# Stick-breaking attention scores as three one-pass products of split q and k, and value products placed behind another block's scores

## The chip, the core and the metric

The kernel runs on one core of a Trainium2 chip. The metric is the device time of one execution in microseconds (us). Below, PE is the matrix engine (TensorE), PEld its weight loads, DVE the vector engine, ACT the scalar engine, POOL GpSimd, and SP the queue that issues the transfers (DMA).

## What is computed

One decoder layer: RMSNorm, an input projection, two groups of 16 heads side by side (a state-space group, SSD, and a stick-breaking attention group), an output projection, and a convolutional feed-forward part. There are 16 meta tokens and 1024 real ones, and all data is float32. The change touches only the attention group, with head width 64:

```python
zlog = einsum('bqhd,bkhd->bhqk', q_block, k) / sqrt(64)
log_beta = log_sigmoid(zlog)
log_keep = where(valid, log_beta - zlog, 0)          # log(1 - beta)
after    = cumsum(log_keep, reverse) - log_keep      # keys between s and t
w        = where(valid, exp(log_beta + after), 0)    # strictly causal
out      = einsum('bhqk,bkhd->bqhd', w, v)
```

The kernel works on probabilities and not on their logarithms: `kp` is sigmoid(-z), `bt` is sigmoid(z), a running product of `kp` from the right end gives the remaining stick, and the weight is `bt` times that product.

## The kernel before

**Matrix products.** A float32 operand is multiplied in one of two ways. In most of the kernel it is split in two float32r parts, the rounded value ("h", written by ACT) and the rest ("l", a subtraction on DVE or POOL), and three products h·h, l·h, h·l are added in PSUM; one of these is one pass over the moving columns. Small products take the float32 tiles as they are. The projections (`pj_...`, line 163) are of the first kind, with 128 contraction rows, and the scores `z` (L612), the transposes `tw` (L633) and the value products `av` (L647) of the second.

**Attention.** Heads are taken in eight pairs p = 0 to 7; the two heads of a pair lie on partitions 0 to 63 and 64 to 127. For each pair there are eight blocks i = 0 to 7 of 128 queries, and block i sees n = 16 + 128(i+1) keys. A block goes through five steps:

- `block_weights`: the scores in chunks of at most 512 keys (widths 144, 272, 400, then 2x264, 2x328, 2x392, 2x456, and 348+348+344 for i = 7). In one chunk, the product of head 0 uses partitions 0 to 63 and that of head 1 partitions 64 to 127. ACT makes `kp` and `bt` out of PSUM (L613, L614), DVE runs the two product scans (L617), and POOL multiplies (L619). The PSUM tiles `zz`, two in all, hold the chunks of `z` and also the transposes `tw`.
- `block_turn`: two blocks later, `bt` is transposed on PE (`tw`) and copied by ACT to `th` (L635).
- `block_mix`: one block later still, the value products `av` of the two heads, 64 output columns each (L647), and the copy to `ysc`.
- once for each pair, `edge_turn` and `edge_mix` (`twc`, `avc`) treat the keys at the block borders.
- between these stand steps of `fill`: the projections of the next pair's q, k and v. A step is half a projection chunk, 12 products, and at most three steps stand in one block. From the middle of pair 6 on there is no `fill` left, and steps of the output projection (`mo`, L783) stand there in some blocks.

In the loop over p and i, the order on PE is the order of the code (`manual_schedule` for PE alone). In it a block reads: scores of its first two chunks; one to three `fill` steps; the third chunk (i = 7 only); `block_mix` of an older block; `block_turn` of an older block; a `fill` step. The other engines' orders are set by the scheduler. The attention tiles lie in a pool `ap`, opened when the SSD part is closed, in memory which that part used until then; whoever first writes there waits for the last SSD transfers. In the SSD part, and through its end, the first pairs' projections already run.

Of the kernel before, what the change touches and what calls it, by code (L numbers as in the profile page):

```python
# [16 lines left out]
P = 128  # L17
# [3 lines left out]
NM = 16  # L21
L = NM + T
# [4 lines left out]
NT = T // P  # L27
# [24 lines left out]
def tile_layer(ctx: ExitStack, tc: tile.TileContext, x, meta, rows, parts,  # L52
               w_z, w_xbc, w_dt, w_q, w_k, w_v, w_out, w_up, w_down, out):
    nc = tc.nc
    mm = nc.tensor.matmul
# [139 lines left out]
    rp = roll.enter_context(tc.tile_pool(name="roll", bufs=2, side="right"))  # L195
# [5 lines left out]
    with tc.tile_pool(name="pre", bufs=3, side="right") as pre:  # L201
        gpre = row_bcast(pre, 0, D, "gpre")
        for i in range(NT + 1):
            nr = NM if i == 0 else P
            c0 = 0 if i == 0 else NM + (i - 1) * P
# [5 lines left out]
            r = rstd_of(pre, ss[:nr], 1, nr, f"pre{i}")  # L211
# [3 lines left out]
            for hf in range(2):  # L215
# [11 lines left out]
    halves = (slice(0, 64), slice(64, 128))  # L227
# [22 lines left out]

    def qkv_steps(p, post):
        q = rp.tile([P, L + 3], F32, tag="rq", name=f"q{p}", bufs=3)
        k = rp.tile([P, L], F32, tag="rk", name=f"k{p}", bufs=3)
        for dst, nm in ((q, "q"), (k, "k")):
            def ev(acc, c0, n, dst=dst):
                nc.scalar.activation(dst[:, c0:c0 + n], acc[:, :n], AF.Copy)

            yield from qkv_block(f"{nm}{p}", ev, p > 1 or (p, nm) == (1, "k"))
        vt = rp.tile([P, L], F32, tag="rt", name=f"vt{p}", bufs=1)

        def evv(acc, c0, n):
# [4 lines left out]
        heads[p] = q, k, v, vc  # L266
        yield from qkv_block(f"v{p}", evv, p > 0)

        def turn_v(part):
            tp = psum_tp(f"vtp{p}_{part}")  # L270
            for b in range(4):
                c0 = (4 * part + b) * P
                nc.tensor.transpose(tp[:, b, :], vt[:, c0:c0 + P], ident)
            nc.scalar.activation(v[:, 4 * part:4 * part + 4, :], tp, AF.Copy)

        def turn_edge():
            edge = rp.tile([P, NT, NM], F32, tag="edge", name=f"edge{p}", bufs=1)
            nc.vector.tensor_copy(edge[:, :NT - 1, :], vt[:, P:NT * P].rearrange("p (t c) -> p t c", c=P)[:, :, :NM])
            nc.vector.tensor_copy(edge[:, NT - 1, :], vt[:, T:L])
            tp = psum_tp(f"vtc{p}")  # L280
            nc.tensor.transpose(tp[:, 0, :], edge.rearrange("p t c -> p (t c)"), ident)
            nc.scalar.activation(vc, tp[:, 0, :], AF.Copy)
            for j in range(2):
                nc.vector.tensor_copy(meta_q[halves[j], p, 4 * p + 2 * j:4 * p + 2 * j + 2], q[halves[j], M0:NM])
            nc.vector.tensor_copy(meta_k[:, p, :], k[:, 0:NM])
            nc.sync.dma_start(out=mvd[:, p, :], in_=v[:NM, 0, :])

        post += [lambda: turn_v(0), lambda: turn_v(1), turn_edge]
# [17 lines left out]
    with tc.tile_pool(name="ssd", bufs=1, side="right") as sp:  # L306
# [114 lines left out]
        q, adt = e, s2  # L421
# [170 lines left out]
                                pattern=[[-NM * mul, NT], [col, 32]], channel_multiplier=mul)  # L592
    edges, ys_of = {}, {}

    def block_weights(p, i):
        q, k = heads[p][:2]
        nm = f"{p}_{i}"
        if i == 0:
            edges[p] = ap.tile([P, 2, NT, NM], F32, tag="cb", name=f"cb{p}", bufs=2)
            nc.gpsimd.memset(edges[p][:, :, :, NM - 1:], 0.0)  # L600
        t0, n = NM + i * P, NM + (i + 1) * P
        kpt = ap.tile([P, 2, L], F32, tag="kp", name=f"kp{nm}", bufs=2)
        btt = ap.tile([P, 2, L], F32, tag="bt", name=f"bt{nm}", bufs=3)
        kp, bt = kpt[:, :, 0:n], btt[:, :, 0:n]
        chunks = key_chunks(n)
        for ci, (a, w) in enumerate(chunks):
            if ci == 2:
                yield
            z = psum_zz(f"z{nm}_{ci}")
            for j in range(2):  # L610
                h = halves[j]
                mm(z[:, j, :w], q[h, t0:t0 + P], k[h, a:a + w], start=True, stop=True)  # L612
            nc.scalar.activation(kp[:, :, a:a + w], z[:, :, :w], AF.Sigmoid, scale=-QSCALE)  # L613
            nc.scalar.activation(bt[:, :, a:a + w], z[:, :, :w], AF.Sigmoid, scale=QSCALE)  # L614
        m = n - NM
        for j in range(2):
            nc.vector.tensor_tensor_scan(kp[:, j][:, ::-1], kp[:, j][:, ::-1], hold[:, L - n:L][:, ::-1], 0.0,  # L617
                                         op0=ALU.mult, op1=ALU.max)
            nc.gpsimd.tensor_tensor(bt[:, j, 0:m], bt[:, j, 0:m], kp[:, j, 1:m + 1], op=ALU.mult)  # L619
        nc.gpsimd.tensor_tensor(edges[p][:, :, i, 0:NM - 1], bt[:, :, m:n - 1], kp[:, :, m + 1:n], op=ALU.mult)  # L620
        turn.append((p, i, bt))
# [188 lines left out]
    for p in range(8):  # L810
        for i in range(NT):
            if p == 0 and i == 0:
                run(fill, 1)
            block = block_weights(p, i)
            next(block, None)
            if p > 0 and i == 3:
                edge_mix(p - 1, edge)
            run(fill, 1 + (i < 3))
            if p == 6 and i == 4:
                ahead = [raw_w(0, k, None if k % 3 == 0 and k < 6 else wp_f32(("wlo", "whi", "wlo")[k % 3], f"wora{k}"))  # L820
                         for k in range(8)]
            run(block)
            if mix:
                block_mix(*mix.pop(0))
            if len(turn) > 2:
                mix.append(block_turn(*turn.pop(0)))
            run(fill, int(p > 0 or i > 3))
            if p == 6 and i == 5:
                run(fill)
                xpool.close()  # L830
                w1pool = wo1.enter_context(tc.tile_pool(name="wo1", bufs=1, side="left"))
                wres = []
                halo = psum_mm("halo0")
                wsteps = wout_steps(w1pool, 0, ssd_g, wres, halo_y(w1pool, 0, ssd_g), halo, ahead)
            if p == 6 and i == 6:
                run(wsteps)
                halo_store(w1pool, 0, halo)
                ys1 = [split_y(wp, 0, 1, ("whi", "wlo", WB))]
                first = ssd_half(wres, ys1)
            elif p == 6 and i == 5:  # L840
                run(wsteps, 4)
            run(first, int(p == 7 and (i % 2 or i > 5) or p == 6 and i == 7))
            if p == 7 and 2 < i < 6:
                run(meta_steps, 1)
            if p == 0 and i == 2:
                token_rstd(r_ssd, ap, "a")
            if p > 0 and i == 2:
                edge = edge_turn(p - 1)
# [808 lines left out]
```

## Time and profile before

| | |
|---|---|
| median of three runs | 1810.84 us (1809.62 to 1811.23) |
| the profiled execution | 1810.72 us |
| its span, first to last instruction | 1809.0 us |
| outside the span | 1.72 us |
| mean granted PE clock | 0.988 |

The page gives for each engine its busy time. Groups of rows name a line, an engine, an operation, output and inputs, and the tile's partitions and elements. In the views by time a row has the start, the length, the engine, the line, the operation, and the number of instructions merged in it; in brackets stands how long the engine was idle before it, and what ended that. Matrix instructions overlap each other, so the distance from start to start says what one costs, and its length does not. A float32 product has two MATMUL records, a float32r product has one. The time from about 420 to 975 us is the attention.

### The profile page before, as it was taken

To read this page: it belongs to the slowest core of one execution; us is meant where nothing else is said; L and a number is where in the kernel's file an instruction comes from. 1 tells how busy PE (TensorE), PEld (TensorE's weight loads), DVE (VectorE), ACT (ScalarE), POOL (GpSimd) and SP (SyncE) were. 2 spreads that over 40 slices of the span, in tenths; PEclk is the share of its full clock that TensorE was granted. 3 is DMA by queue.
4 is the path that set the end of the run, shared out by engine and by line. 5 is a ranking of instruction groups with operands and counts; after the bars stand their busy time and mean duration, and the time that the engine had idled before them with its cause. 6 is when DMAs were issued, how large, how long until landed. Compare 5 with 4: busy or idle time off the path is not lost. (4 is left out here: it accounts for less than half of the span.)

```text
span 1809.0 us, 27308 instructions
## 1 busy us (share of the span) xinstructions
PE 1734.8 (96%) x10942; PEld 1490.1 (82%) x10942; DVE 1061.0 (59%) x1125; ACT 831.3 (46%) x1373; POOL 863.3 (48%) x613
## 2 busy tenths in 40 slices
PE   6999999999999999999889899899999999999997
PEld 5899889888888888887567578888899998888886
DVE  5651864873553454455731246766666666657988
ACT  5423563544565565565652334543333333344444
POOL 3213753585555565554752223277777776600001
PEclk9999999999999999999999899999999999999999
DMA  4124333231011011011212545222333332196344
GB/s 157 47 71 131 99 114 118 65 94 42 24 37 36 26 46 36 24 48 61 70 54 76 200 140 174 73 97 88 105 111 105 93 112 88 60 327 220 97 122 158
DMA packets 90547, 173.96 MB, mean 96 GB/s; under 512 B 10698, under 2 KB 35818, under 8 KB 90420
## 3 DMA queue, kind: packets, MB, share of 16 engines
q1 hardware_dynamic: 90420, 172.21, 29.7%
q8 instruction: 86, 1.41, 0.3%
q14 instruction: 41, 0.34, 0.1%
HBM read 122.39 MB, written 49.79 MB: 95 GB/s over the span
## 5 line engine op out<-in xcount | busy, mean ns | idle before, releaser
L617 DVE TENSOR_TENSOR_SCAN kp<-kp,hold 128x272 f32<-128x272 f32 (+7 forms) x128 | 206.8, 1657 | 194.7 <-ACT kp L613 104.5
L619 POOL TENSOR_TENSOR bt<-bt,kp 128x256 f32<-128x256 f32 (+7 forms) x128 | 215.0, 1697 | 189.2 <-DVE kp L617 132.9
L1022 POOL TENSOR_TENSOR wl<-wr,wh 128x1024 fp32r<-128x1024 f32 x44 | 110.7, 2524 | 40.7 <-ACT wh L1021 40.7
L1470 PE MATMUL dn<-dl,dh 128*128 128x512 f32 x308 | 119.9, 389 | 0.1
L1470 PE MATMUL dn<-dh 128*128 128x512 f32 x308 | 119.9, 389 | 0.0
L1470 PE MATMUL dn<-dh,dl 128*128 128x512 f32 x308 | 119.8, 389 | 0.0
L1516 POOL TENSOR_TENSOR fms<-fms,nhalf 128x1 f32<-128x1 f32 x8 | 8.5, 1060 | 225.7 <-DMA ar<-fda 186.0
L613 ACT ACTIVATE kp<-z 128x288 f32<-128x288 f32 (+6 forms) x112 | 82.8, 739 | 56.8 <-PE z L612 33.1
L1399 ACT ACTIVATE dh<-ar 128x512 fp32r<-128x512 f32 x77 | 48.7, 632 | 111.5 <-PE dn L1470 88.9
L612 PE MATMUL z<-k,q 64*128 64x144 f32 (+6 forms) x448 | 87.0, 488 | 13.3 <-ACT bt L614 6.0
L1021 ACT ACTIVATE wh<-wr 128x1024 fp32r<-128x1024 f32 x44 | 46.6, 1060 | 114.7 <-PE fX L1079 68.3
L1151 DVE SCALAR_TENSOR_TENSOR ga<-gr,pp,ga 128x1024 f32<-128x1024 f32 x44 | 71.3, 1622 | 34.8 <-ACT ga L1144 34.0
L635 ACT ACTIVATE th<-tw 128x1024 f32<-128x1024 f32 (+2 forms) x96 | 74.7, 814 | 34.9 <-PE tw L633 33.0
L614 ACT ACTIVATE bt<-z 128x288 f32<-128x288 f32 (+6 forms) x112 | 83.0, 741 | 0.0
L633 PE MATMUL tw<-ident,bt 128*128 128x128 f32 x576 | 78.8, 282 | 3.8 <-issue 2.8
L647 PE MATMUL av<-th,v 128*64 128x128 f32 x1152 | 78.3, 281 | 0.0
L647 PEld LDWEIGHTS av<-th,v 128*64 128x64 f32 x1152 | 62.8, 138 | 18.8 <-issue 17.9
L1400 DVE TENSOR_TENSOR dl<-ar,dh 128x512 fp32r<-128x512 f32 x77 | 53.3, 692 | 42.0 <-ACT dh L1399 42.0
L633 PEld LDWEIGHTS tw<-ident,bt 128*128 128x128 f32 x576 | 63.2, 143 | 15.6 <-issue 13.1
L612 PEld LDWEIGHTS z<-k,q 64*128 64x128 f32 x448 | 36.9, 187 | 41.8 <-issue 18.5
L1470 PEld LDWEIGHTS dn<-dh 128*128 128x128 f32 x308 | 57.8, 188 | 12.3 <-ACT dh L1399 0.3
L1470 PEld LDWEIGHTS dn<-dl,dh 128*128 128x128 f32 x308 | 57.8, 188 | 12.3 <-DVE dl L1400 0.4
(546 smaller groups left out, 5749.2 us busy)
## 6 DMA issues: line engine op xcount, KB each, us to landing
wr<-in_w_up SPq DMA_DIRECT2D x44, 512.0 KB
fds<-ga SPq DMA_DIRECT2D x44, 256.0 KB
b<-in_w_down SPq DMA_DIRECT2D x44, 256.0 KB
ar<-fds SPq DMA_DIRECT2D x44, 256.0 KB
fda<-ga SPq DMA_DIRECT2D x33, 256.0 KB
ar<-fda SPq DMA_DIRECT2D x33, 256.0 KB
yk<-yd SPq DMA_DIRECT2D x16, 512.0 KB
zd<-zt SPq DMA_DIRECT2D x8, 520.0 KB
```

The lines of the kernel that those rows point to most:

```text
L612: mm(z[:, j, :w], q[h, t0:t0 + P], k[h, a:a + w], start=True, stop=True)
L613: nc.scalar.activation(kp[:, :, a:a + w], z[:, :, :w], AF.Sigmoid, scale=-QSCALE)
L614: nc.scalar.activation(bt[:, :, a:a + w], z[:, :, :w], AF.Sigmoid, scale=QSCALE)
L617: nc.vector.tensor_tensor_scan(kp[:, j][:, ::-1], kp[:, j][:, ::-1], hold[:, L - n:L][:, ::-1], 0.0, op0=ALU.mult, op1=ALU.max)
L619: nc.gpsimd.tensor_tensor(bt[:, j, 0:m], bt[:, j, 0:m], kp[:, j, 1:m + 1], op=ALU.mult)
L633: nc.tensor.transpose(tw[:, j, b, :], bt[:, j, c0:c0 + P], ident)
L635: nc.scalar.activation(th[:, :, :nb, :], tw[:, :, :nb, :], AF.Copy)
L647: mm(av[halves[j], :], v[:, kb, halves[j]], th[:, j, b, :], start=kb == 0, stop=kb == i)
L1022: nc.gpsimd.tensor_tensor(l, raw, h.bitcast(F32), op=ALU.subtract)
L1151: nc.vector.scalar_tensor_tensor(v, self.g[jj][:, :, i:i + 256], fconv_w[:, j, i:i + 1], v, op0=ALU.mult, op1=ALU.add)
L1400: sub(lo[:, k], raw, hi[:, k].bitcast(F32), op=ALU.subtract)
L1470: mm(banks[t], u[:, 0, c], v[:, 1, :], start=(p == 0 and i == 0), stop=(p == NPR - 1 and i == 2))
```

## The change

Three things are changed.

- k is written by ACT as a float32r tile `kh`, and DVE subtracts it from the projection's PSUM tile to make `kl` (L259 of the new file): three subtractions for each pair. The copy of the meta keys becomes a sum of the two.
- For every block, DVE makes `qh` (a cast, L604) and `ql` (a subtraction, L605) of the block's 128 queries. This is issued one block ahead, behind the scores of the block before; for block (0, 0) it is issued at its start. The tiles lie in the pool `ap`.
- The scores of a chunk are three one-pass products for each head (qh·kh, ql·kh, qh·kl), the two heads in turn. `block_mix` stands directly behind the first two chunks of scores, ahead of `edge_mix` and the `fill` steps; it stood behind the whole block.

```diff
-        k = rp.tile([P, L], F32, tag="rk", name=f"k{p}", bufs=3)
-        for dst, nm in ((q, "q"), (k, "k")):
+        kh = rp.tile([P, L], F32R, tag="rk", name=f"kh{p}", bufs=3)
+        kl = rp.tile([P, L], F32R, tag="rkl", name=f"kl{p}", bufs=3)
+        for dst, nm in ((q, "q"), (kh, "k")):
             def ev(acc, c0, n, dst=dst):
                 nc.scalar.activation(dst[:, c0:c0 + n], acc[:, :n], AF.Copy)
+                if dst is kh:
+                    nc.vector.tensor_tensor(kl[:, c0:c0 + n], acc[:, :n], kh[:, c0:c0 + n].bitcast(F32), op=ALU.subtract)
...
-            nc.vector.tensor_copy(meta_k[:, p, :], k[:, 0:NM])
+            nc.vector.tensor_tensor(meta_k[:, p, :], kh[:, 0:NM].bitcast(F32), kl[:, 0:NM].bitcast(F32), op=ALU.add)
...
+    def split_q(p, i):
+        q = heads[p][0][:, NM + i * P:NM + (i + 1) * P]
+        qh = ap.tile([P, P], F32R, tag="qh", name=f"qh{p}_{i}", bufs=2)
+        ql = ap.tile([P, P], F32R, tag="ql", name=f"ql{p}_{i}", bufs=2)
+        nc.vector.tensor_copy(qh, q)
+        nc.vector.tensor_tensor(ql, q, qh.bitcast(F32), op=ALU.subtract)
+        qsplit[p, i] = qh, ql
+
     def block_weights(p, i):
-        q, k = heads[p][:2]
+        kh, kl = heads[p][1]
+        if (p, i) not in qsplit:
+            split_q(p, i)
+        qh, ql = qsplit.pop((p, i))
...
-            for j in range(2):
-                h = halves[j]
-                mm(z[:, j, :w], q[h, t0:t0 + P], k[h, a:a + w], start=True, stop=True)
+            for s_, (u, r) in enumerate(((qh, kh), (ql, kh), (qh, kl))):
+                for h, j in zip(halves, range(2)):
+                    mm(z[:, j, :w], u[h, :], r[h, a:a + w], start=s_ == 0, stop=s_ == 2)
...
+        nxt = (p, i + 1) if i < NT - 1 else (p + 1, 0)
+        if nxt[0] in heads:
+            split_q(*nxt)
...
             next(block, None)
+            if mix:
+                block_mix(*mix.pop(0))
             if p > 0 and i == 3:
                 edge_mix(p - 1, edge)
...
             run(block)
-            if mix:
-                block_mix(*mix.pop(0))
             if len(turn) > 2:
                 mix.append(block_turn(*turn.pop(0)))
```

In order on PE, the last block of a pair (here block 7 of pair 4, with the `fill` products left out between the groups) reads before:

```order
L612 MATMUL z4_7_0_6965<-k4_5558,q4_5557 128x348 x2
L612 MATMUL z4_7_1_6970<-k4_5558,q4_5557 128x348 x2
L612 MATMUL z4_7_2_6988<-k4_5558,q4_5557 128x344 x2
L647 MATMUL av4_4_6998<-th4_4_0_6943,v4_5974 64x128 x8
L647 MATMUL av4_4_6998<-th4_4_1_6948,v4_5974 64x128 x2
L633 MATMUL tw4_5_0_7010<-ident_69,bt4_5_6817 128x128 x8
L633 MATMUL tw4_5_1_7021<-ident_69,bt4_5_6817 128x128 x4
```

Twelve projection products stand between the second and the third row. The same place on PE after the change, where they stand between the rows of `av` and those of the third chunk:

```order
L628 MATMUL z4_7_0_7418<-kh4_5822,qh4_7_7355 128x348 x2
L628 MATMUL z4_7_0_7418<-kh4_5822,ql4_7_7356 128x348 x2
L628 MATMUL z4_7_0_7418<-kl4_5823,qh4_7_7355 128x348 x2
L628 MATMUL z4_7_1_7427<-kh4_5822,qh4_7_7355 128x348 x2
L628 MATMUL z4_7_1_7427<-kh4_5822,ql4_7_7356 128x348 x2
L628 MATMUL z4_7_1_7427<-kl4_5823,qh4_7_7355 128x348 x2
L666 MATMUL av4_4_7436<-th4_4_0_7396,v4_6304 64x128 x8
L666 MATMUL av4_4_7436<-th4_4_1_7401,v4_6304 64x128 x2
L628 MATMUL z4_7_2_7461<-kh4_5822,qh4_7_7355 128x344 x2
L628 MATMUL z4_7_2_7461<-kh4_5822,ql4_7_7356 128x344 x2
L652 MATMUL tw4_5_0_7479<-ident_69,bt4_5_7246 128x128 x8
L652 MATMUL tw4_5_1_7490<-ident_69,bt4_5_7246 128x128 x4
```

The value products have moved from behind the third chunk to ahead of the projections, so the transposes now follow the third chunk of scores (its third product, kl with qh, is not shown). At the start of the attention, DVE's order before is this (`zk` is the last SSD product, `hold` the first tile that DVE writes in `ap`):

```order
L542 TENSOR_TENSOR zk1_8_3922<-yt1_8_3961,zk1_8_3922 128x512
L585 MEMSET hold_3990 128x520
L300 MEMSET tmsa_4169 128x1
L687 COPY pick_8537<-identb_74 16x32
L586 CAST hold_3990<-ident_69 128x128
L617 SCALAR_TENSOR_TENSOR kp0_0_4031<-kp0_0_4031,hold_3990 128x144 x2
```

and after the change it is this:

```order
L545 TENSOR_TENSOR zk1_8_3927<-yt1_8_3966,zk1_8_3927 128x512
L588 MEMSET hold_3995 128x520
L604 CAST qh0_0_4034<-q0_3077 128x128
L589 CAST hold_3995<-ident_69 128x128
L605 TENSOR_TENSOR ql0_0_4035<-q0_3077,qh0_0_4034 128x128
```

The split of the first queries stands behind the filling of `hold`, and PE's first scores, which read nothing from the pool `ap` before, now read `qh` and `ql`.

More of the change, by code (lines that the diff above doesn't have):

```diff
@@ L265, in qkv_steps @@
         vc = rp.tile([P, P], F32, tag="vc", name=f"vc{p}")
-        heads[p] = q, k, v, vc
+        heads[p] = q, (kh, kl), v, vc
         yield from qkv_block(f"v{p}", evv, p > 0)
@@ L593, in tile_layer @@
     edges, ys_of = {}, {}
+    qsplit = {}
+    def split_q(p, i):
[5 more added lines that the diff above has]
+        qsplit[p, i] = qh, ql
     def block_weights(p, i):
-        q, k = heads[p][:2]
+        kh, kl = heads[p][1]
         nm = f"{p}_{i}"
+        if (p, i) not in qsplit:
+            split_q(p, i)
+        qh, ql = qsplit.pop((p, i))
         if i == 0:
@@ L600, in block_weights @@
             nc.gpsimd.memset(edges[p][:, :, :, NM - 1:], 0.0)
-        t0, n = NM + i * P, NM + (i + 1) * P
+        n = NM + (i + 1) * P
         kpt = ap.tile([P, 2, L], F32, tag="kp", name=f"kp{nm}", bufs=2)
```

## Prediction

> **What bounds the kernel.** I read the page's engine list first, then busy time by stretch (columns: length, then PE, PEld, DVE, ACT, POOL with counts, the granted PE clock, DMA share, GB/s).
>
> ```profile
> PE 1734.8 (96%) x10942; PEld 1490.1 (82%) x10942; DVE 1061.0 (59%) x1125; ACT 831.3 (46%) x1373; POOL 863.3 (48%) x613
> ...
> 350.00:360.00 10.00, 9.51 (x72) 7.63 (x70) 9.49 (x11) 5.93 (x14) 8.65 (x7) 1.00 0.42 117
> 595.00:663.00 68.00, 67.71 (x517) 57.15 (x516) 31.08 (x24) 38.52 (x66) 37.64 (x29) 1.00 0.11 32
> 860.00:870.00 10.00, 6.38 (x54) 2.91 (x50) 10.00 (x6) 9.90 (x16) 7.78 (x5) 1.00 0.24 87
> 870.00:880.00 10.00, 6.96 (x38) 5.38 (x39) 10.00 (x5) 8.32 (x15) 9.77 (x4) 0.66 0.00 0
> ```
>
> PE is the bound as a whole. The second stretch is about one pair's worth of the attention: PE busy in 67.71 of 68 us, DVE, ACT and POOL at 45 to 57%. There a nanosecond on PE is a nanosecond of the end, and DVE has room. Two places differ. At 860 to 880 (pair 6, blocks 4 to 7, no `fill` left) DVE is full and PE is not; at the end of the SSD part (first stretch) DVE and PE are both nearly full.
>
> What a product costs is read from start to start, in time order (start, length, engine, line):
>
> ```profile
> 644.55 0.32 PE L163 MATMUL pj_v<-xh,wl_v 128*128 128x346 f32 x1
> 644.80 0.55 PE L612 MATMUL z<-k,q 64*128 64x328 f32 x2
> 645.18 0.44 PE L612 MATMUL z<-k,q 64*128 64x328 f32 x2
> 645.46 0.44 PE L612 MATMUL z<-k,q 64*128 64x328 f32 x2
> 645.74 0.44 PE L612 MATMUL z<-k,q 64*128 64x328 f32 x2
> 646.11 0.43 PE L163 MATMUL pj_v<-xh,wh_v 128*128 128x346 f32 x1
> 646.38 0.32 PE L163 MATMUL pj_v<-xl,wh_v 128*128 128x346 f32 x1
> 646.53 0.32 PE L163 MATMUL pj_v<-xh,wl_v 128*128 128x346 f32 x1
> ...
> 1233.15 2.89 PE fX L1079 x24
> ```
>
> Each z row is one record of both heads, so the two heads run side by side. A step of it is 0.28 us for 328 columns. At 2.4 columns per ns two passes would be 0.273, so a float32 record is two passes and almost nothing else, and a chunk (two records) is four. A split product of 346 columns (646.38 to 646.53) takes 0.15 to 0.16 us against 0.144 for one pass; the group of 24 products in the last row, from the chain of waits, has 258 columns and takes 0.120 each against 0.1075. So a one-pass product costs its columns plus some 14 ns.
>
> **A. The scores, pass by pass.** Before, a chunk of w columns costs 4w/2.4 + 6 ns; after, three one-pass products a head, side by side, 3(w/2.4 + 14) ns. The saving is w/2.4 minus 36 ns. On the PE-bound path lie pairs 0 to 5 and blocks 1 to 3 of pair 6: 82 chunks over 144 columns, 28752 columns together. 28752/2400 = 11.98 us, minus 82 x 0.036 = 2.95, gives +9.0 (plus is gain). The seven chunks of 144 columns are bound by their loads at 0.108 a step (the spacing of `tw` below), three steps against 0.246, so they lose 0.5. Pair 7's 13 wide chunks are partly off the path: half of their 1.5, +0.7. Sum +9.2. With an overhead of 3 ns, as in the float32 step, it would be +11.9; with 20 ns, +7.7.
>
> The Trainium skill ("TensorE: Matmul & The Clock Gate", Part 1) gives the gap between warm matmuls as N/2.4 plus about 2.5 ns; 82 x 3 x 0.0115 = 2.8 us more would then be gained. The trace's 0.120 at 258 columns disagrees with it, and the 0.28 of the float32 step agrees; which holds for one-pass products on half the rows no row here shows.
>
> **B. Changes of the array's split.** A change between 128 rows and two halves costs something on both sides. From 644.55 to 644.80 is 0.25 where 0.16 is usual, the first z step is 0.38 instead of 0.28, and the first `pj` behind (646.11 to 646.38) 0.27 instead of 0.16: about 0.09 ahead and 0.10 behind, 0.20 for a change into z or into `pj`.
>
> ```profile
> 647.96 0.32 PE L163 MATMUL pj_v<-xh,wl_v 128*128 128x346 f32 x1
> 648.21 0.33 PE L647 MATMUL av<-th,v 128*64 128x128 f32 x2
> 648.80 0.33 PE L633 MATMUL tw<-ident,bt 128*128 128x128 f32 x1
> 648.96 0.71 PE L633 MATMUL tw<-ident,bt 128*128 128x128 f32 x5
> ...
> 639.26 0.65 PE L667 MATMUL avc<-thc,vc 128*64 128x256 f32 x4
> 639.84 0.43 PE L163 MATMUL pj_v<-xh,wh_v 128*128 128x346 f32 x1
> 640.11 0.32 PE L163 MATMUL pj_v<-xl,wh_v 128*128 128x346 f32 x1
> ```
>
> Into `av` it is 0.14 (0.09 ahead, then 0.05), from `av` into `tw` 0.15 (648.80 to 648.96 is 0.16, and further `tw` steps are 0.109). A block has pj-z 0.20, z-pj 0.20, pj-av 0.14, av-tw 0.15 = 0.69. After, it has pj-z 0.20, z-av 0.15 (the place at 604.06 below), av-pj 0.20 (639.84 to 640.11, as behind z) and pj-tw, both 128 rows, nothing: 0.55. That is 0.145 saved in each of 37 blocks, and twice that in the six blocks with i = 3 of pairs 1 to 6, where `av` comes to stand directly before `avc`: 5.4 + 1.7 = +7.1. In the last blocks (i = 7) the count of changes is the same. From below 0: if `av` has to wait for `th`, which is now needed earlier. ACT is at 57% there and `th` was asked for two blocks later than its `tw`; I find its copies done at least 0.65 us ahead of the new place, so I take 7.1.
>
> **C. Block 7: what covered the buffer.** There are two PSUM tiles `zz`. Before, `av` (10 products a head) stood between the third chunk and the transposes.
>
> ```profile
> 603.28 0.85 PE L612 MATMUL z<-k,q 64*128 64x344 f32 x4
> 604.06 1.31 PE L647 MATMUL av<-th,v 128*64 128x128 f32 x20
> 605.30 0.33 PE L633 MATMUL tw<-ident,bt 128*128 128x128 f32 x1
> ...
> 604.17 0.74 ACT L613 ACTIVATE kp<-z 128x688 f32<-128x688 f32 x1 [0.75 <-PE z L612]
> 604.82 0.74 ACT L614 ACTIVATE bt<-z 128x688 f32<-128x688 f32 x1
> ```
>
> The third chunk's tile is free when `bt` ends, 605.56. Now the eight transposes of the first half follow z at once: start 604.06, 0.05 + 8 x 0.109 = 0.92, done at 604.98; the four of the second half need that tile and wait 0.58, with the 0.1 that a hand-over takes (604.06 to 604.17) some 0.65. That the whole chain starts 0.1 earlier shifts both. Six pairs: -3.9 (0 if other work comes between, -4.5 with 0.75 each).
>
> **D. The first scores.** Before, z of block (0, 0) waited for nothing, while DVE sat:
>
> ```profile
> 419.98 0.52 PE L612 MATMUL z<-k,q 64*128 64x144 f32 x4
> 420.42 0.43 PE L163 MATMUL pj_k<-xh,wh_k 128*128 128x348 f32 x1
> ...
> 423.91 0.49 DVE L585 MEMSET hold<- 128x520 uint32 x1 [5.15 <-DMA yd<-zk]
> 424.43 0.49 DVE L586 CAST hold<-ident 128x128 bf16<-128x128 f32 x1
> ```
>
> DVE stands 5.15 us at `hold`, its first tile in the pool `ap`, until an SSD transfer ends. `qh` and `ql` are in that pool and stand behind `hold` on DVE. They are two operations of 128x128, priced by
>
> ```profile
> L224 DVE TENSOR_TENSOR xl<-xtp,xh 128x512 fp32r<-128x512 f32 x16 | 9.9, 679 | 0.6 <-ACT xh L223 0.6
> L486 DVE TENSOR_TENSOR cbm<-cb,tri 128x128 f32<-128x128 f32 x16 | 4.5, 284 | 3.2 <-PE cb L484 3.1
> ```
>
> at 0.28 each beside `hold`'s own 0.49: `ql` ends near 425.4, and the projection behind z resumes at about 425.75 where it was 420.42, as PE is in order. Loss 5.3, with nothing to take back. The gap has a second price. The stretch 870 to 880 has a granted clock of 0.66, so 6.8 us at half speed:
>
> ```profile
> 872.32 1.52 PE L612 MATMUL z<-k,q 64*128 64x344 f32 x4 [4.72 <-ACT bt L614]
> ...
> 879.83 0.50 PE L783 MATMUL mo<-woha,yl 128*128 128x512 f32 x1 [0.72 <-POOL yl L773]
> ```
>
> That dip follows 4.72 us in which PE stood still; at the start PE would stand about 4.9 in a PE-bound part, where 6.8 us at half speed cost 3.4. I take 2.5 of it, since the gaps are alike. Together -7.8 (-5.0 to -8.9).
>
> **E. DVE in the SSD part.** The projections of pairs 0 and 1 run there, so some `kl` subtractions (0.679 x 346/512 = 0.46 each) fall where DVE is at 9.49 of 10. PE is at 9.51 beside it and most delays find other products: -0.5 (0 to -1.4, three of them in full).
>
> **F. The tail of pair 6.** In 860 to 880 DVE is the bound. The splits of four blocks (0.5 to 0.6 each, cast and subtraction) go in front of the scans there, while the shorter scores give back 0.3. `mo` already waits for `yl` at 879.83, and what is late on DVE is late there. Four splits are 2.2, about 1.3 of it in the chain: -1.0 (-2 to +2). Elsewhere 21 more `kl` and some 60 splits are free: DVE has 37 of 68 us idle in a pair, and a split is issued a block ahead of its use. Without that cover they'd cost a pair 8 x 0.55.
>
> **Sum.** +9.2 + 7.1 - 3.9 - 7.8 - 0.5 - 1.0 = +3.1 against the profiled execution's 1810.72 (1809.0 span and 1.72 around it), which lies 0.12 below the median: 1807.6, I say 1807.5. A measurement tells about 0.2% from no change, so "faster" is below 1807.2 and "slower" above 1814.5. Own range, with one bound of A, C or D at a time and F: 1803 to 1812.
>
> **Rivals.**
>
> *R1, only the columns count.* One-pass products on halves cost 3 ns beside their columns like the float32 records, and the idle time at the start leaves the clock alone: +2.7 and +2.5, 1802. For it: the z steps themselves; against it: all other one-pass rows. Chance 0.14.
>
> *R2, the loads come into sight (slower).* A chunk now has three loads of each head instead of two, and the pass that hides one is 0.14 us long, not 0.28. If a load onto the rows of a running product had to wait for its end, each of 246 steps would cost the load's 0.10 (the spacing that the first z step shows) in place of the 0.014: 246 x 0.086 = 21 lost, 1828.5. From 28 ns more a step on it outweighs 3.1 + 3.8 us and decides the sign. Against it: z steps of 0.28 leave no room for an open load, and `pj` steps of 0.16 hide theirs. Chance 0.09. The Trainium skill (same page, Part 3, "What overlaps and what doesn't") says that weight loads overlap running matmuls only where the row group differs, which speaks for R2; the 0.28 from 645.18 to 645.46, on the same rows, disagrees.
>
> *R3, more waits than C and D.* The scores now hang on DVE (`ql` behind scans, some 60 times), and a projection's PSUM tile is held until DVE has taken `kl`, not only until ACT has copied. From 0.1 us a block on, 48 blocks cost 5, which with the sum is 1812.5; 0.2 gives 1817. For it: scans of over a microsecond stand in DVE's queue; against it: DVE's idle half. Chance 0.22.
>
> *R4, no stall at the start* (the tile's wait is over earlier than I read): +7.8, 1800. Chance 0.05.
>
> **Chances.** My forecast 0.50, split by the bound at 1807.2 nearly in the middle: 0.23 faster, 0.27 same. R1 and R4 are faster (0.19), R2 slower (0.09), R3 0.08 same, 0.14 slower. So faster 0.42, same 0.35, slower 0.23. The range 1800 to 1817 leaves out R2 and the ends of the others.
>
> **What the profile after would show.** A: z steps of about 0.151 us at 328 columns, three a chunk; 0.139 for R1, over 0.2 for R2. B: `av` starts 0.09 behind the last z step, and `tw` follows `pj` with no gap. C: `tw` of the second half waiting some 0.65 for ACT `bt` in block 7 of pairs 0 to 5. D: PE idle near 420 to 425 before z, released by DVE `ql`, and a slice of half clock behind it. E, F: DVE busy up by some 45 us, nearly all beside PE. The forecast is wrong if z waits for `ql` in later blocks, or if a projection waits for DVE `kl`.

## The result, and the profile after

The changed kernel takes 1812.51 us (median; 1811.12 to 1815.62) where the kernel before, timed beside it, takes 1810.89. The ratio is 1.0008 (95% interval 1.0000 to 1.0015): no difference by the 0.2% bound, and if one, a loss of 1.6 us where the sum had a gain of 3.1. The profiled execution took 1812.49 us, 1810.8 of them span.

The page of the changed kernel, and its busy time by stretch (length, PE, PEld, DVE, ACT, POOL, granted PE clock, DMA share, GB/s):

```profile
PE 1723.7 (95%) x11166; PEld 1512.3 (84%) x11166; DVE 1121.2 (62%) x1277; ACT 828.7 (46%) x1373; POOL 858.3 (47%) x613
...
595.00:663.00 68.00, 67.18 (x560) 61.00 (x560) 43.29 (x45) 39.68 (x67) 39.62 (x30) 1.00 0.12 35
860.00:870.00 10.00, 5.73 (x58) 3.38 (x58) 9.96 (x8) 9.88 (x16) 7.17 (x4) 1.00 0.17 55
870.00:880.00 10.00, 4.28 (x20) 3.12 (x20) 9.97 (x5) 6.61 (x12) 9.89 (x4) 0.55 0.00 0
880.00:890.00 10.00, 10.00 (x58) 7.95 (x59) 6.55 (x6) 2.63 (x5) 7.30 (x4) 0.77 0.17 53
```

PE is busy for 11 us less, yet the span is longer. In a pair PE remains the bound (67.18 of 68 us). New is the last row: PE full at a granted clock of 0.77. Before, that stretch had full clock. The half clock lay in 870 to 880 (0.66, so 6.8 us of it), on products behind which PE still waited for `yl` (0.72 us at 879.83), so it cost little there. Now 0.55 and 0.77 make 13.6 us of half clock in the two rows:

```profile
880.00:890.00 10.00, 9.48 (x69) 7.47 (x69) 5.29 (x4) 4.57 (x8) 7.88 (x4) 1.00 0.18 55
```

The same sequence of PE as in the prediction, scores of a block and the value products behind them:

```profile
647.96 0.42 PE L628 MATMUL z<-kh,qh 64*128 64x328 f32 x2
648.22 0.32 PE L628 MATMUL z<-kh,ql 64*128 64x328 f32 x2
648.37 0.32 PE L628 MATMUL z<-kl,qh 64*128 64x328 f32 x2
648.53 0.31 PE L628 MATMUL z<-kh,qh 64*128 64x328 f32 x2
648.67 0.31 PE L628 MATMUL z<-kh,ql 64*128 64x328 f32 x2
648.82 0.31 PE L628 MATMUL z<-kl,qh 64*128 64x328 f32 x2
649.06 0.66 PE L666 MATMUL av<-th,v 128*64 128x128 f32 x8
...
608.11 0.43 PE L628 MATMUL z<-kh,qh 64*128 64x344 f32 x2
608.37 0.33 PE L628 MATMUL z<-kh,ql 64*128 64x344 f32 x2
608.53 0.33 PE L628 MATMUL z<-kl,qh 64*128 64x344 f32 x2
608.79 1.09 PE L652 MATMUL tw<-ident,bt 128*128 128x128 f32 x8
```

The two heads still run side by side, a pass of 328 columns takes 0.14 to 0.16 us, and no load shows: step A is right, R1 (0.139) and R2 (over 0.2) are out.

Where the time went is read best from the moment at which PE starts the first score of a block, in both traces:

| first score of block (pair, block) | before | after | after minus before |
|---|---|---|---|
| (0, 1) | 424.45 | 432.04 | +7.59 |
| (0, 3) | 436.21 | 443.60 | +7.39 |
| (0, 4) | 440.38 | 448.92 | +8.54 |
| (2, 0) | 540.61 | 546.54 | +5.93 |
| (4, 0) | 676.75 | 679.51 | +2.76 |
| (6, 3) | 841.83 | 840.35 | -1.48 |
| (6, 7) | 866.16 | 863.88 | -2.28 |
| (7, 0) | 885.30 | 887.55 | +2.25 |
| (7, 7) | 942.77 | 944.61 | +1.84 |
| end of the span | 1809.0 | 1810.8 | +1.8 |

The start costs 7.6. From there to (6, 3) the change earns 9.1 us, some 1.8 in most pairs. Between (6, 7) and (7, 0), where pair 6 runs out of projections, 4.5 us are lost, and the lead with them. The start, in PE's and DVE's rows:

```profile
424.89 0.48 PE L628 MATMUL z<-kh,qh 64*128 64x144 f32 x2 [5.30 <-DVE qh L604]
425.96 0.66 PE L163 MATMUL pj_k<-xh,wh_k 128*128 128x348 f32 x1
426.42 0.49 PE L163 MATMUL pj_k<-xl,wh_k 128*128 128x348 f32 x1
...
424.08 0.49 DVE L588 MEMSET hold<- 128x520 uint32 x1 [5.78 <-DMA yd<-zk]
424.49 0.20 DVE L604 CAST qh<-q 128x128 fp32r<-128x128 f32 x1
```

PE stood 5.30 us, and then its products took 0.29 us apiece (426.42 to 426.71 further on) in place of 0.16: half clock. The tail of pair 6:

```profile
870.03 0.43 PE L628 MATMUL z<-kh,qh 64*128 64x344 f32 x2 [3.69 <-ACT bt L630]
874.31 1.12 PE L652 MATMUL tw<-ident,bt 128*128 128x128 f32 x4 [1.00 <-ACT bt L630]
875.07 0.78 PE L802 MATMUL mo<-woha,yh 128*128 128x512 f32 x1
879.94 0.80 PE L802 MATMUL mo<-woha,yl 128*128 128x512 f32 x1 [4.09 <-POOL yl L792]
880.53 0.63 PE L802 MATMUL mo<-wola,yh 128*128 128x512 f32 x1
880.96 0.63 PE L802 MATMUL mo<-woha,yh 128*128 128x512 f32 x1
...
877.61 2.36 DVE L604 CAST qh<-q 128x128 fp32r<-128x128 f32 x1
...
876.55 3.33 POOL L792 TENSOR_TENSOR yl<-yk,yh 128x1024 fp32r<-128x1024 f32 x1
```

Before, `mo` with `yl` started at 879.83 after a wait of 0.72, and went on so:

```profile
880.16 0.39 PE L783 MATMUL mo<-wola,yh 128*128 128x512 f32 x1
880.39 0.40 PE L783 MATMUL mo<-woha,yh 128*128 128x512 f32 x1
```

Now PE comes early, waits 4.09 and starts at 879.94: the lead of 2.28 us was gone by then, as `yl` on POOL is no earlier. And the products behind it take 0.43 us (880.53 to 880.96) instead of 0.23 until 884.4: some ten of them, 2.1 us. Also, one cast takes 2.36 us. Three questions follow. Is it the splits on DVE that keep `yl` late, or is a lead simply worth nothing there? Does the half clock on `mo` come of the wait? And what makes the cast so long?

### The profile page after: what moved, and what is told of

It is laid out like the page before. It is cut to its first block, busy times and chain, and to the rows that moved or that the text cites. A ratio compares the mean times of both kernels' runs of the same rounds, so it can differ in the third digit from the quotient of the medians.

```text
span 1810.8 us, 27925 instructions
## 1 busy us (share of the span) xinstructions
PE 1723.7 (95%) x11166; PEld 1512.3 (84%) x11166; DVE 1121.2 (62%) x1277; ACT 828.7 (46%) x1373; POOL 858.3 (47%) x613
## 5 line engine op out<-in xcount | busy, mean ns | idle before, releaser
L636 DVE TENSOR_TENSOR_SCAN kp<-kp,hold 128x272 f32<-128x272 f32 (+7 forms) x128 | 185.7, 1491 | 29.4 <-ACT kp L629 21.9
L1535 POOL TENSOR_TENSOR fms<-fms,nhalf 128x1 f32<-128x1 f32 x8 | 8.5, 1060 | 225.7 <-DMA ar<-fda 186.0
L1040 ACT ACTIVATE wh<-wr 128x1024 fp32r<-128x1024 f32 x44 | 46.6, 1060 | 114.9 <-PE fX L1098 68.3
L604 DVE CAST qh<-q 128x128 fp32r<-128x128 f32 x64 | 38.5, 601 | 90.4 <-PE z L628 90.1
L1489 PEld LDWEIGHTS dn<-dl,dh 128*128 128x128 f32 x308 | 57.8, 188 | 12.5 <-DVE dl L1419 0.4
L1489 PEld LDWEIGHTS dn<-dh,dl 128*128 128x128 f32 x308 | 57.8, 188 | 12.0
```

The costliest lines, as they stand in the source:

```text
L1489: mm(banks[t], u[:, 0, c], v[:, 1, :], start=(p == 0 and i == 0), stop=(p == NPR - 1 and i == 2))
```

## The experiments

In the following, "lead" is how much earlier than in the kernel before (its first trace) the first score of a block starts.

### Each half of the change alone, two inputs for the cast, and an earlier first split

Two theories stand against each other. T1: the casts of q hold DVE up in pair 6's tail. T2: DVE and POOL set the time there, whatever PE does before.

e1 keeps the value products in their old place:

```diff
             next(block, None)
-            if mix:
-                block_mix(*mix.pop(0))
...
             run(block)
+            if mix:
+                block_mix(*mix.pop(0))
```

> The scores are split as in the changed kernel, the value products stay in their old place. Both theories expect the lead over the kernel before, at the start of block 3 of pair 6, to change from 1.5 us to a lag of about 1.7 (no switches saved, 7.1; no wait of the transposes in block 7, 3.9 back). Theory T1 (the tail of pair 6 is late because the casts of q wait on DVE; a lead or lag on PE before it is passed on): 1815 to 1816.5. Theory T2 (at the tail of pair 6 DVE and POOL set the time whatever PE does before, so a lead is worth nothing): 1811.5 to 1813.5, like the changed kernel.

Measured: 1819.35 us (ratio 1.0047, 1.0032 to 1.0062). It comes to (6, 3) with a lead of 0.02 (the start cost 6.5 here, and a pair earned 1.3), loses 4.8 at the tail, 2.3 in pair 7 and 2.3 more behind the attention, the latter two in half-clock stretches. Neither total was right. What holds is the price by blocks: 0.20 us is gained in block 4, 0.24 in block 5, 0.28 in block 6 and 0.32 in block 7, against 0.20, 0.25, 0.31 and 0.33 by step A.

e2 is the opposite, the kernel before with this:

```diff
             next(block, None)
+            if mix:
+                block_mix(*mix.pop(0))
...
             run(block)
-            if mix:
-                block_mix(*mix.pop(0))
```

> The scores are those of the kernel before, only the value products are moved. Both theories: a lead of about 3 us at block 3 of pair 6 (7.1 of switches less 3.9 of waits in block 7), no stall at the start. T1: no casts, so the lead is kept: about 1808. T2: the lead is lost where mo waits for yl in pair 6: 1810 to 1811.

Measured: 1810.43 us (ratio 1.0001, 0.9992 to 1.0011). Each block earned 0.15 us and block 3 0.29, as step B said; block 7 lost 0.67 in each pair (0.65 forecast), and 1.02 in one. There is no split, and `mo` with `yl` started 0.58 before the kernel before's, with the lead of (6, 7), 0.57, intact: T2 is wrong, though the total is the one that it gave. But the next products took 0.43 us each, and 2.8 us were lost by (7, 0):

```profile
879.25 0.80 PE L783 MATMUL mo<-woha,yl 128*128 128x512 f32 x1 [2.32 <-POOL yl L773]
879.84 0.63 PE L783 MATMUL mo<-wola,yh 128*128 128x512 f32 x1
880.27 0.63 PE L783 MATMUL mo<-woha,yh 128*128 128x512 f32 x1
```

So the half clock on `mo` needs no splits. Moving the value products is enough: they used to stand between PE's long wait for the third chunk's buffer and `mo`, and without them the wait for `yl` grew from 0.72 to 2.32.

e3 makes `qh` with an instruction of two inputs:

```diff
-        nc.vector.tensor_copy(qh, q)
+        nc.vector.tensor_tensor(qh, q, q, op=ALU.max)
```

> The changed kernel, with qh made by a DVE operation of two inputs (the maximum of q and q) in place of the cast. T1: the 64 operations take 0.28 to 0.30 us each, whether POOL is at work or not (the casts' mean is 0.60, up to 2.5 where POOL is at work); the tail's DVE chain ends 2 to 4 us earlier, mo waits less for yl: 1808.5 to 1810.5. T2: 1812 to 1813, since the chain is bound by the scans and POOL's own products.

Measured: 1812.64 us (ratio 1.0010, 1.0001 to 1.0020). The group of `qh` in the changed kernel, and then in e3 (form, count, busy time, mean ns):

```profile
L604 DVE CAST qh<-q 128x128 fp32r<-128x128 f32 x64 | 38.5, 601 | 90.4 <-PE z L628 90.1
```

```profile
L604 DVE TENSOR_TENSOR qh<-q 128x128 fp32r<-128x128 f32 x64 | 40.6, 635 | 89.4 <-PE z L628 89.2
```

The two-input form is no cheaper, so T1 in its narrow form, that the cast is the culprit, is wrong. The rows show a regularity. In both kernels `qh` takes 0.20 to 0.29 us when POOL is idle. Where a POOL product of tensors in SBUF is under way, it nearly always ends 0.08 (cast) or 0.15 us (maximum) after that product's end, however long that is: the cast at 877.61 above ends at 879.97, POOL's `yl` at 879.88. The kernel before already shows it, on DVE and POOL:

```profile
745.99 1.90 DVE L285 COPY meta_k<-k 128x16 f32<-128x16 f32 x1
...
744.00 6.05 POOL L619 TENSOR_TENSOR bt<-bt,kp 128x1024 f32<-128x1024 f32 x2 [2.33 <-DVE kp L617]
```

A copy of 16 columns took 1.90 us, where another copy of that line takes 0.14.

e4 puts the tiles `qh`, `ql` in the pool of q and splits block (0, 0) ahead of `ap`:

```diff
-        qh = ap.tile([P, P], F32R, tag="qh", name=f"qh{p}_{i}", bufs=2)
-        ql = ap.tile([P, P], F32R, tag="ql", name=f"ql{p}_{i}", bufs=2)
+        qh = rp.tile([P, P], F32R, tag="qh", name=f"qh{p}_{i}", bufs=2)
+        ql = rp.tile([P, P], F32R, tag="ql", name=f"ql{p}_{i}", bufs=2)
...
+    split_q(0, 0)
     apool = ExitStack()
```

> The changed kernel, with the tiles qh and ql in the pool of q (same sizes), and the split of the first block issued ahead of the pool ap: z of block (0, 0) then waits for nothing. Both theories: PE's stall of 5.3 us and the half clock behind it (2.5) are gone, a lead of about 9 us at block 3 of pair 6. T1: most of it is kept, 1804 to 1806.5. T2: it is lost at the tail of pair 6, 1811 to 1812.5.

Measured: 1808.32 us (ratio 0.9984, 0.9974 to 0.9993). The start's 7.6 us are gone (lead 0.09 at (0, 1)), the lead at (6, 3) is 8.5, and 4.5 of it are left at (7, 0). A lead is passed on, less the tail's 4.7; the total lies between the two forecasts. Another 2.3 go in block 5 of pair 7, at half clock:

```profile
912.00:922.00 10.00, 8.07 (x54) 5.99 (x51) 6.99 (x9) 6.78 (x12) 4.21 (x5) 0.68 0.08 28
```

### Undoing the parts that cost

T3: a PE that comes early to the tail stands idle for `yl`, and the half clock that follows falls on `mo`. e5 leaves the value products of block 7 where they were:

```diff
-            if mix:
+            if mix and i < NT - 1:
                 block_mix(*mix.pop(0))
...
             run(block)
+            if mix and i == NT - 1:
+                block_mix(*mix.pop(0))
```

> The changed kernel, but in the last block of each pair the value products stand in their old place, between the third chunk and the transposes. If the transposes' wait for the buffer in block 7 costs what the step of the sum says, each of pairs 0 to 5 gains 0.65 to 0.75 us there: 4 to 4.5 in all. Theory T3 (a PE that comes early to the tail of pair 6 stands idle for yl, and the half clock that follows falls on the mo products): PE's idle time ahead of mo is shorter, as the value products and transposes stand there, so 2 more are saved: 1806 to 1807. Rival (the lead is given back in another half-clock stretch): 1808.5 to 1811.

Measured: 1811.60 us (ratio 1.0002, 0.9992 to 1.0012). Step C stands: block 7 earns 0.34 us where the changed kernel loses 0.35, and the pair with the 0.8 loss earns 0.24; from (0, 1) to (6, 3) that is 4.4 us. The total shows 0.9 of it, since the tail still lost 4.8: PE's wait for `yl` was still 3.74 us, so the 2 us that T3 had expected there were not saved; and block 5 of pair 7 cost 2.4 at half clock.

e10 only changes the order of the first output step's products:

```diff
+            prods = [(u, v, k) for k, (wh, wl) in enumerate(w) for u, v in ((yh, wh), (yl, wh), (yh, wl))]
+            if half == 0 and t == 1 and hf == 0:
+                prods = [x for x in prods if x[0] is yh] + [x for x in prods if x[0] is yl]
...
```

> The changed kernel, but in the first half of the first output-projection step (pair 6, block 7) the sixteen products of yh stand ahead of the eight of yl: same products, another order. T3: PE no longer waits 4.1 us for yl after its first product, and does its half-clock stretch on work that it would have done later: z of block (7, 0) comes 4 to 5.6 us earlier; 1808 to 1809.5. Rival (what follows in pair 7 is set by POOL and DVE, or the idle time moves to the next wait): 1811.5 to 1813.

Measured: 1811.83 us (ratio 0.9997, 0.9988 to 1.0007).

```profile
876.71 0.78 PE L804 MATMUL mo<-woha,yh 128*128 128x512 f32 x1
877.29 0.63 PE L804 MATMUL mo<-wola,yh 128*128 128x512 f32 x1
...
879.37 0.39 PE L804 MATMUL mo<-woha,yh 128*128 128x512 f32 x1
...
881.67 2.08 PE L804 MATMUL mo<-woha,yl 128*128 128x512 f32 x8
883.68 0.33 PE L628 MATMUL z<-kh,qh 64*128 64x144 f32 x2
```

With work in place of the wait the clock is back at 879.4, and between (6, 7) and (7, 0) this kernel gains 1.0 us where the changed one loses 4.5: 5.5 of the 4 to 5.6 expected. T3 holds for the place. The total is the rival's: in this execution the attention began 1.7 later than in the changed kernel's, and block 5 of pair 7 lost 2.7 at half clock. The ten times spread from 1806.43 to 1813.66 us, and the two shortest have the highest mean granted clock, 0.985 and 0.986 against 0.979 in the profiled execution.

e6 splits q where k is split, out of PSUM, into one `ql` tile for each block (kh and kl have two buffers each, for room):

```diff
-        nc.vector.tensor_copy(qh, q)
-        nc.vector.tensor_tensor(ql, q, qh.bitcast(F32), op=ALU.subtract)
...
+                for i in range(NT):
+                    a, e = max(c0, NM + i * P), min(c0 + n, NM + (i + 1) * P)
+                    if a < e:
+                        o_ = a - NM - i * P
+                        nc.vector.tensor_tensor(ql[i][:, o_:o_ + e - a], acc[:, a - c0:e - c0], qh[:, a:e].bitcast(F32), op=ALU.subtract)
...
```

> q is split where k is: ACT writes qh out of PSUM, and DVE subtracts it from PSUM, ten subtractions for each pair into one tile ql for each block; no cast and no split from SBUF is left (for room, kh and kl have two buffers each). T1: the stall of the first scores (7.6 with its half clock) goes, and so does what the splits cost in the tail of pair 6 (1.7, the difference between the runs with and without splits): 1803 to 1804.5. Rival (the lead is given back in half-clock stretches, as the early split of the first block kept 4.3 of 7.6): 1806 to 1808. DVE's subtractions out of PSUM take the same time whether POOL is at work or not.

Measured: 1810.25 us (ratio 0.9995, 0.9986 to 1.0005), above both forecasts. The two local claims hold: block (0, 1) starts with a loss of 0.26 only, and the tail costs 2.7, as in e2, instead of 4.5. What the splits cost in the tail is read best from the chain that makes `yl`. From the first score of (6, 3) to the end of `yl` it takes 37.95 us in the kernel before, 37.94 in e2 and 37.96 in e6, but 39.54 in the changed kernel, and 39.5 to 39.8 in e1, e3, e4, e5 and e10, which all split q on DVE out of SBUF. So the splits cost 1.6 us there, and without them a lead reaches `yl` in full. The other 2.1 us of the changed kernel's loss fall behind `yl`: from `mo` with `yl` to the first score of (7, 0) it takes 7.61 us instead of 5.47. DVE's subtractions from PSUM are short:

```profile
L269 DVE TENSOR_TENSOR ql<-pj_q,qh 128x128 fp32r<-128x128 f32 x48 | 11.6, 279 | 7.9 <-PE z L626 7.9
```

But of a lead of 8.0 at (6, 3), 5.2 are left at (7, 0), 3.0 at (7, 7), and 1.1 at the end.

e13 takes the last three edits together: block 7's old place, `yh` first, and the split out of PSUM.

> The last three edits together: q split at its projection, block 7's value products in the old place, yh ahead of yl in the first output step. If the gains add: 7.6 + 1.7 + 4.2 + 3 below the changed kernel, 1796. If the leads are partly given back in half-clock stretches and in pair 7's waits: 1799 to 1803.

Measured: 1804.17 us (ratio 0.9965, 0.9953 to 0.9977), faster than both kernels, though above both forecasts. The lead is 12.1 at (6, 3), 11.9 at (7, 0), 9.3 at (7, 7) and 7.8 at the end: the tail is mended, pair 7 isn't.

### Which half-clock stretches belong to the change

Half-clock stretches come up at other places in nearly every trace. Three kernels were profiled once more: the kernel before, the changed one, and e2.

> The kernel before once more, for a second profiled execution. Theory T4 (where a half-clock stretch falls depends on where the idle time of PE falls in the throttle's own count of time, so it differs from execution to execution of the same kernel): the stretches in the attention differ from the first profile's, above all near 440 (none in the first), at mo in pair 6 and at block 6 of pair 7. Rival T5 (they belong to the order of the kernel): the same stretches at the same places, to 1 us.

> The changed kernel once more. T5: half clock again at 424 to 428, 444 to 447, and 873 to 884 (two stretches, the second on the mo products, 2.1 us), none at block 6 of pair 7. T4: at least one of these is at another place or missing, and the span moves by 1 to 3 us with it; the shares of the time that are no stretches (steps of z 0.151 at 328 columns, gains of 0.27 to 0.45 in blocks 1 to 6 of a pair) stay to 0.02.

> The run with the value products moved and the scores as before, once more, as its first profile (1813.65) lay above its median (1810.4). T4: the stretch on mo in pair 6 or that near 440 is missing, which takes 1.2 to 2.8 us off. T5: the same stretches.

The kernel before (span 1810.5) now has a stretch from 437.0 to 440.4, which the first trace did not have, and it costs 1.5 us there; after it, the distance of the two traces changes by 0.07 us at most from block to block through to the last. The first row is of its first trace, the two below of the second.

```profile
430.00:440.00 10.00, 10.00 (x72) 8.98 (x71) 3.27 (x6) 5.95 (x11) 6.49 (x5) 1.00 0.14 51
```

```profile
430.00:440.00 10.00, 10.00 (x62) 9.07 (x60) 3.98 (x6) 5.02 (x9) 6.95 (x6) 0.85 0.19 54
440.00:450.00 10.00, 10.00 (x65) 7.21 (x65) 3.47 (x3) 6.23 (x12) 6.48 (x6) 0.98 0.00 0
```

So such a stretch can come without the change (T4), and it costs the changed kernel the same 1.5 us: it lost 1.16 between (0, 3) and (0, 4), where it earns 0.39 in the next pair. But that the change has no part in it isn't shown: every trace with the change or a part of it has this stretch, and of the kernel before's only the second. The changed kernel's second trace (span 1812.1) repeats the tail: 4.51 us, a wait of 4.08 for `yl`, products of 0.43. That is its own (T5). Its start was 1.4 later, with a stretch at 340 in the SSD part. In e2 the tail cost 1.3 instead of 2.8: after the same wait, 5 products of `mo` take 0.43 us, where it was 13. So both theories hold, each for its places. In the tail it goes, in the main, by the length of PE's wait for `yl`:

| wait of `mo` for `yl`, us | in | products of `mo` behind it |
|---|---|---|
| 0.72, 1.78 | the kernel before, two executions | 0.23 us each |
| 0.92 | e15 (below) | 0.23 us each |
| 1.68, 1.90 | e6, e12 (below) | 0.43 us each at first |
| 2.32, 2.31 | e2, two executions | 0.43 us each at first |
| 3.74, 3.99, 4.01, 4.17 | e5, e1, e4, e3 | 0.43 us each at first |
| 4.09, 4.08 | the changed kernel, two executions | 0.43 us each at first |

Either part of the change alone makes the wait long enough: the moved value products (e2) and the splits (e1, where the value products stand in their old place).

Two things more can be read from the traces. In each trace the granted clock changes only at points of one grid of 3.41 us, and the stretches of half clock are one to four such windows long. This explains the row of the table that doesn't fit, 1.68 with half clock against 1.78 without: in e6 the clock is halved from 864.0 to 877.7, since the longer wait for the third chunk's buffer, and the wait for `yl` (to 871.88) lies inside (it is the same in e12, from 870.7 to 884.3); in the second trace of the kernel before, that earlier stretch ended at 877.3, before the wait began. And the stretch in block 5 of pair 7, which costs 2.3 to 2.9 us where it comes, goes by how the grid cuts PE's idle time just ahead of it: the emptiest window there has PE busy for 0.54 to 0.56 of its length in the seven traces with the stretch (e1, e4, e5, e6, e10, e12, e13), and for 0.58 to 0.64 in the seven without (both traces of the kernel before, of the changed one and of e2, and e3). As a threshold this holds for that place only: a window of `mo` and its wait, with PE busy for 0.48 (877.3 to 880.7 in the second trace of the kernel before), has no half clock behind it.

e14 adds to e13 a step of the output projection in every block of pair 7:

```diff
-            run(first, int(p == 7 and (i % 2 or i > 5) or p == 6 and i == 7))
+            run(first, int(p == 7 or p == 6 and i == 7))
```

> The kernel with q split at its projection, block 7's value products in the old place and yh first, and beside that one step of the output projection in every block of pair 7 (it was every second one), so that PE has work in place of its waits there. If those waits are what sets pair 7's length: 1800 to 1803. If yl on POOL comes too late for the denser steps: 1804 to 1808.

Measured: 1787.53 us (1782.46 to 1791.85; ratio 0.9871, 0.9844 to 0.9898), 12.5 us below the lower end. From 880 to 1060 us, first in the kernel before and then here:

```profile
880.00:1060.00 180.00, 164.77 (x966) 125.83 (x967) 54.47 (x53) 70.02 (x106) 68.45 (x47) 0.96 0.34 112
```

```profile
880.00:1060.00 180.00, 170.54 (x1011) 134.13 (x1010) 67.23 (x70) 77.38 (x120) 71.19 (x51) 0.98 0.38 125
```

PE's waits of pair 7 are filled, fewer output steps are left behind the attention, and the clock stays up (1.00 from 865 to 1052).

### What the subtraction waits for, and whose gain e14's is

e12 casts `qh` on ACT:

```diff
-        nc.vector.tensor_copy(qh, q)
+        nc.scalar.activation(qh, q, AF.Copy)
```

> The changed kernel, with qh cast by ACT in place of DVE; the subtraction ql stays on DVE. Theory T1 (a DVE instruction with its operands in SBUF starts only when the POOL instruction under way ends): the wait passes to ql, whose mean grows from 0.39 us to 0.5 to 0.7, and the tail of pair 6 gains under 1 us. Rival (the cast itself is the dear one, as a copy of one operand): ql stays at 0.29 where POOL is at work, and z of block (7, 0) comes 1.5 us earlier or more.

Measured: 1818.28 us in one execution. The mean of `ql` went from 540 ns (0.39 in the text above was too low) to 1142, beyond the range named:

```profile
L605 DVE TENSOR_TENSOR ql<-q,qh 128x128 fp32r<-128x128 f32 x64 | 34.6, 540 | 2.0
```

```profile
L605 DVE TENSOR_TENSOR ql<-q,qh 128x128 fp32r<-128x128 f32 x64 | 73.1, 1142 | 0.2 <-ACT qh L604 0.2
```

Where POOL was at work, `ql` ended 0.15 us after POOL's product. So the wait is not the cast's: before, the cast had waited first. T1 holds in its wide form, for DVE instructions with their operands in SBUF. The tail gained 0.4 us from (6, 3) to (7, 0), under 1 as T1 said, and the chain to `yl` took 38.91: 1.0 longer than without splits, not 1.6. The loss in total came in pair 7 (4.9 us from (7, 0) to (7, 7)); it was not followed up.

e15 is the kernel before with e14's last edit alone (the same diff).

> The kernel before with one step of the output projection in every block of pair 7. If the gain of that edit comes from PE's waits in pair 7 and behind the attention and has nothing to do with the split scores: 1810.8 less some 12 to 17, 1794 to 1799. If it needs the lead that the other edits gave (the weights' halves and yl come too late otherwise): 1803 to 1811.

Measured: 1800.28 us (ratio 0.9948, 0.9931 to 0.9964), between the two forecasts. So some 10 us of e14's gain (10.2 against the median beside it, 1810.52) have nothing to do with the change. The other 12.7 (1800.28 to 1787.53) are what split scores and moved value products are worth with their costs mended, against 1.6 of loss as they came; they hold what `yh` first would bring by itself, which was not run without the change.

## Why the prediction was right and wrong

A gain of 3.1 us was forecast and a loss of 1.6 measured: wrong by 4.7 us of 1810, and in sign. The sum's own range of 1803 to 1812 misses the time, 1812.51; only the wide one, 1800 to 1817, holds it, by way of R3's waits, which did not come. The upper end of the own range doesn't follow from its terms either: 1807.6 with A's low bound and F's makes 1810.1. "Faster" had the highest chance, 0.42, and "no change" came.

In the traces the loss is 1.8 us, 4.9 away from the sum: 2.7 in step F, 1.5 in the half-clock stretch near 440, for which the sum had no term, 0.6 that A, B, C and E fall short, and 0.3 in pair 7, less 0.2 gained on D.

- **A, the passes: right.** One pass costs its columns plus 13 to 15 ns on half the rows too. Three one-pass products a head stay side by side. The Trainium skill's 2.5 ns (TensorE: Matmul & The Clock Gate, Part 1) does not fit these steps; nor does its rule that loads overlap only onto other rows (Part 3), as 0.15 us for a step is the pass of 0.137 and 0.013 beside it, which leaves no room for an open load.
- **B, the switches: right**, 0.15 us a block and 0.29 in block 3 (e2). A, B, C and E together were to bring 11.2 us up to the tail (+9.2 less pair 7's 0.7, +7.1, -3.9, -0.5); the trace has 9.1, or 10.6 without the stretch near 440 that the kernel before has too in one of its traces.
- **C, block 7: right, a little small**: 4.4 measured (e5), 3.9 forecast, 4.5 the bound. One pair pays 1.0 instead of 0.67, as ACT has weights and q to copy ahead of z there.
- **D, the start: right**, 7.6 for 7.8, and in its parts: 4.9 of stall (424.89 for 419.98) and 2.7 behind it, for 5.3 and 2.5; e4 takes all of it away.
- **E** cannot be told from what differs from run to run: the attention's start differs by 1 to 2 us between executions of one kernel.
- **F, the tail of pair 6: this is the step that failed.** It was put at -1.0 (down to -2) and is -3.7, counted from (6, 3) to (7, 0); from (6, 7) it is -4.5. It had the chain right (splits, scans, POOL, `yl`, `mo`), and the splits' share of it nearly: 1.6 us against 1.3, though its price for one split, 0.5 to 0.6 us from rows with POOL idle, was half of what was measured (601 and 540 ns in the mean for cast and subtraction, and up to 2.5 us for one beside POOL), and DVE's busy time rose by 60 us instead of 45. What it put at nothing is PE's clock: 2.1 us. The half clock of 870 to 880 was taken from the profile as a price for the start, but not asked of the tail, where it had fallen ahead of a wait and so cost little. With PE early and the wait for `yl` at 4.09 us, it lasts on into `mo`. The loss is there without any split (2.8 and 1.3 us in e2's two traces, where the chain to `yl` takes no longer than before), and is gone when the order gives PE work in place of the wait (e10).
- **Pair 7**: +0.7 forecast, +0.4 measured.
- **The rivals.** R3 had the nearest total, 1812.5, by the wrong waits, so that is luck: behind the first one no z waited for `qh` or `ql` (0.15 us or more), and no projection for `kl`. R1, R2 and R4 are out.

Open is what, beside PE's idle time, decides on the half clock: the stretch near 440 follows a window in which PE was busy throughout, in both kernels.

## What to carry to other kernels

A gain on a bound engine is worth what the next place leaves of it: follow the lead from stage to stage, by the start of the same piece of work in both traces, and ask at each place whether the engine that comes early only waits, and whether its clock falls while it waits. Where a wait can't be removed, put independent products into it (e10's order, e14's steps) before shortening the work ahead of it. And price a small DVE operation by its rows beside a busy POOL, or take its operand from PSUM.

## What the runs showed of the hardware

- DVE waits for POOL on SBUF. A cast or copy within SBUF, a subtraction or a scan, met by a POOL product under way, ended 0.03 to 0.15 us (scans: their own length) after it; a cast of 0.23 us took up to 2.49, while `kl`, with one operand in PSUM, took 0.52 whether POOL was at work or not. The Trainium skill says this: the pair of ports that DVE and GpSimd share is an exclusive lock (Trainium Architecture — The Big Picture, "What this means for kernel authors"), and instructions with two SBUF inputs contend as well as two-port copies (GPSIMD Engine Reference, "Key points"). The traces agree in both.
- The half clock comes in pieces of some 3.4 us: 0.85 and 0.98 over two stretches of 10 us in the second trace of the kernel before make 3.4, 0.66 over 870 to 880 makes 6.8, and all changes of the clock in a trace lie on one grid of 3.41 us. The Trainium skill has windows of about 3.4 us that run on regardless of the kernel (TensorE: Matmul & The Clock Gate, Part 1), which fits both the size and that two executions of one kernel differ in where they fall. One such piece moves a span by 1.5 us here, about as much as the whole loss of 1.6 that was to be explained.
